# Attention probabilities turned by VectorE and a trip through memory; layer 1's gate path row-major

## The chip, the cores and the metric

The kernel runs on one NeuronCore of a Trainium2 chip. Its time is the device time of one execution in microseconds (us). TensorE multiplies matrices (a 128x128 stationary operand is loaded, then up to 512 columns stream past it), VectorE and ScalarE work element by element, GpSimd issues DMAs and a few small operations, SyncE issues the weight DMAs. All of them run side by side and wait for each other by semaphores.

## The reference, cut to what matters

A trunk of two layers on 256 tokens of width 2048, all in float32. Each layer is a token mixer, a gate, an output projection, a residual with layer norm, and a gated embedding:

```python
# layer 0: y = sgu_mixer(x, w_in_a)      u * (w_s @ LN(v) + b_s) * silu(z)
# layer 1: y = moba_mixer(x, w_in_b)
q, k, v, z = split(x @ w_in)             # 16 heads of 128
probs = softmax(causal(q @ k.T * 128 ** -0.5))     # 256 keys are one block: plain causal attention
y = (probs @ v) * silu(z)
# both layers
x = layer_norm(alpha * x + y @ w_out)
x = x + sigmoid(x @ w_ple_gate) * (p @ w_ple_proj)
```

With 256 tokens there is one key block, so the block selection of the second mixer drops out.

## The kernel before, in words

**Precision.** Every operand is split into a high part (rounded to TensorE's fp32r form, ScalarE, `split` L75 and L128) and a low part (the rest, VectorE, L76 and L129). A product is made of three matmuls: high by high, low by high, high by low.

**Weights.** They stream once through SBUF in chunks of 128x2048 numbers (1 MB). `load_weights` (L112) lets SyncE load a chunk in two halves and lets ScalarE and VectorE make its high and low part. `weights` (L132) keeps two chunks ready ahead of the one in use; there are three buffers for converted chunks. The list `chunks` (L93 to L108) gives the order and form of the chunks: `flat` for 128 output features by all 2048 inputs, `by_blocks` for 512 output features by 512 inputs.

**Two forms of a projection.** `row_slice` (L237) makes 512 output features for all tokens, token-major: tokens are the stationary operand, weights stream in 512 columns. It takes four `row_unit`s of one chunk each, each unit 24 matmuls of 512 columns (4 input tiles x 2 token tiles x 3). `column_unit` (L244) makes 128 output features feature-major from one chunk: weights are stationary, and the high and low part of the tokens stream. It takes 32 matmuls: 16 of 512 columns (both parts of the tokens at once) and 16 of 256. What follows a token-major result often needs it feature-major, so there are two ways to turn it: `turn` (L269) uses TensorE's transposes, `turn_far` (L283) uses VectorE's transposes of 32x32 blocks and lets two sets of DMAs (GpSimd's queue) put the blocks in place through a DRAM buffer: eight DMAs out, two back.

**Order of work.** The program is written out in one order and each engine executes its instructions in order. Each unit ends with `tick` (L167); `at(n, f, ...)` (L163) puts `f` after the n-th tick from then on. So smaller work lies between the units by tick counts written by hand.

**Layer 1's mixer.** After the values (L627 to L632) come 16 heads (L696): two column units make q and k of a head (`halves_sum`, then `split`). One tick later `scores` (L638) makes the masked scores (five matmuls), the row maxima, the exponentials and the normalised probabilities `sm`, token-major. Two ticks after that `probs` (L667) turns them: three 128x128 transposes on TensorE into a PSUM bank `pt`, then the split into high and low part `pb` (L673, L674). One tick later `values` (L677) multiplies by v and leaves the head's output `o` feature-major. After the heads, 16 column units make z feature-major (L703): two units, `halves_sum`, silu, times `o`, `split` into `br`. Then `after` (L470) multiplies `br` by w_out in four row slices, and so on.

**Layer 0's mixer** makes its z in another way (`gated`, L451): four row slices, silu, times `u`, and `turn_far` for the first three slices.

**Buffers.** `r4` (128x1024 floats) has 12 buffers, `t4` 20, `t2` 5, PSUM 8 banks.

Of the kernel before, what the change touches and what calls it, by code (L numbers as in the profile page):

```python
# [8 lines left out]
F32 = mybir.dt.float32  # L9
F32R = mybir.dt.float32r  # L10
AF = mybir.ActivationFunctionType
ALU = mybir.AluOpType

P = 128
D = 2048
S = 256
KT = D // P
NM = S // P
NS = D // 512
# [16 lines left out]
def f32(ap):  # L36
    return ap.bitcast(F32)
# [3 lines left out]
def decoder_trunk(ctx: ExitStack, tc: tile.TileContext, xT, pT, wv_a, wu_a, wz_a, w_sT, b_s,  # L41
# [5 lines left out]
    nc = tc.nc  # L47
# [4 lines left out]
    dram = ctx.enter_context(tc.tile_pool(name="dram", bufs=1, space=bass.MemoryType.DRAM))  # L52
    psum = ctx.enter_context(tc.tile_pool(name="psum", bufs=8, space=bass.MemoryType.PSUM))

    def t2(name):
        return act.tile([P, 512], F32, name=name, tag="t2", bufs=NT2)

    def t4(name):
        return act.tile([P, 1024], F32R, name=name, tag="t4", bufs=NT4)

    def r4(name):

        return act.tile([P, NM, 512], F32, name=name, tag="r4", bufs=NR4)

    def bank(name):
        return psum.tile([P, 512], F32, name=name, tag="bank", bufs=8)

    def in2(t):
        return t.rearrange("p (i s) -> p i s", i=2)

    def split(src, n="s", g=2):

        t = t4(n).rearrange("p (g h s) -> p g h s", g=g, h=2)
        src = src.rearrange("p (g s) -> p g s", g=g)
        nc.scalar.activation(t[:, :, 0, :], src, AF.Copy)  # L75
        nc.vector.tensor_sub(t[:, :, 1, :], src, f32(t[:, :, 0, :]))  # L76
        return t
# [4 lines left out]
    def by_blocks(w):  # L82

        return [("p (b k c) -> p k b c", dict(b=4, k=4),
                 w[4 * n:4 * n + 4, :, 512 * c:512 * c + 512].rearrange("b p e -> p b e"))
                for n in range(NS) for c in range(4)]

    def flat(src):
        return [("", {}, src.rearrange("p (b e) -> p b e", b=4))]
# [3 lines left out]
    chunks = []  # L93
    for k in range(KT):
        chunks += flat(wv_a[k])
    chunks += by_blocks(wu_a) + by_blocks(wz_a)
    for i in range(DEPTH):
        if i == 1:
            for h in range(2):
                for c in range(KT // 2):  # L100
                    chunks += flat(wv_b[h, c])
            for h in range(KT):
                chunks += flat(wqkz_b[h]) + flat(wqkz_b[KT + h])
            for f in range(KT):
                chunks += flat(wqkz_b[2 * KT + f])
        chunks += by_blocks(w_out[i])
        chunks += flat(w_proj[i, 0]) + flat(w_proj[i, 1])
        chunks += by_blocks(w_gate[i])  # L108
# [33 lines left out]
    ident = consts.tile([P, P], F32, name="ident")  # L142
# [20 lines left out]
    def at(units, f, *args):  # L163

        later.append([units, f, args])
# [71 lines left out]
    def row_slice(xs, name="y"):  # L237

        banks = [[bank(name)] for _ in range(NM)]
        for c in range(4):  # L240
            row_unit(banks, range(4 * c, 4 * c + 4), xs, both if c == 3 else None)
        return [b[0] for b in banks]

    def column_unit(xs, joined=False):  # L244


        ps = bank("f")
        wh, wl = (t.rearrange("p (k c) -> p k c", k=KT) for t in weights()[2:])
        for k in range(KT):
            feature_product(ps, wh[:, k, :], wl[:, k, :], xs, k, joined)  # L250
        tick()
        return ps
# [12 lines left out]
    def halves_sum(o, ps):  # L265
        nc.scalar.activation(o, ps[:, 0:S], AF.Copy)
        nc.vector.tensor_add(o, o, ps[:, S:2 * S])
# [12 lines left out]
        if keep is not None:  # L280
            nc.scalar.activation(keep[j // 2][:, j % 2, :], tp, AF.Copy)

    def turn_far(xs, n, rows, name):  # L283


        d = dram.tile([512, S], F32, name=f"{name}{n}")
        t = r4(name + "b")

        def block_turn():
            for m in range(NM):  # L290
                nc.vector.transpose(t[:, m, :], rows[n][:, m, :])  # L291
            for m in range(NM):
                for g in range(4):
                    c = slice(m * P + 32 * g, m * P + 32 * g + 32)
                    nc.gpsimd.dma_start(d[:, c].rearrange("(b c) t -> c b t", c=32),  # L295
                                        t[32 * g:32 * g + 32, m, :].rearrange("p (b t) -> p b t", t=32))

        def back():
            raw.append(r4(name + "r"))
            for j in range(2):  # L300
                nc.gpsimd.dma_start(in2(raw[0][:, j, :]),
                                    d[j * S:(j + 1) * S, :].rearrange("(u p) t -> p u t", p=P))

        def splits():
            for j in range(2):
                s = split(raw[0][:, j, :], name)
                xs[4 * n + 2 * j:4 * n + 2 * j + 2] = [s[:, u] for u in range(2)]

        raw = []
        block_turn()  # L310
        at(1, back)
        at(4, splits)
# [6 lines left out]
    xs = [None] * KT  # L319
# [125 lines left out]
    for n in range(NS):  # L445
        y = row_slice(xs, "u")
# [4 lines left out]
    def gated(o, xs):  # L451

        br = [None] * KT
        for n in range(NS):
            y = row_slice(xs, "z")
            for m in range(NM):
                t = t2("sz")
                nc.scalar.activation(t, y[m], AF.Silu)
                nc.vector.tensor_mul(o[n][:, m, :], o[n][:, m, :], t)
            if n < NS - 1:  # L460
                turn_far(br, n, o, "bt")
                continue
            for i in range(2):
                at(1 + i, turn, br, 2 * n + i, o, "b")
        return br

    br = gated(us, xs)
# [153 lines left out]
    xs = after(0, br)  # L621
# [12 lines left out]
    o = [None] * NS  # L634
    blocks = (slice(0, P), slice(P, 3 * P))
    w3 = slice(0, 3 * P)

    def scores(h, qk):  # L638
        qh, ql = qk[:, 0, 0, :], qk[:, 0, 1, :]
        kh, kl = qk[:, 1, 0, :], qk[:, 1, 1, :]  # L640
        c0, c1 = slice(0, P), slice(P, S)
        sc = bank("sc")

        t = sc.rearrange("p (a b) -> p a b", b=P)[:, 0:4:3, :]
        nc.tensor.matmul(t, qh[:, c0], qk[:, 1, :, c0], start=True, stop=False, skip_group_check=True)
        nc.tensor.matmul(sc[:, c0], ql[:, c0], kh[:, c0], start=False, stop=True, skip_group_check=True)
        t = sc[:, blocks[1]]
        nc.tensor.matmul(t, qh[:, c1], kh, start=True, stop=False, skip_group_check=True)
        nc.tensor.matmul(t, qh[:, c1], kl, start=False, stop=False, skip_group_check=True)
        nc.tensor.matmul(t, ql[:, c1], kh, start=False, stop=True, skip_group_check=True)  # L650
        s = t2("sm")
        nc.vector.tensor_add(s[:, w3], sc[:, w3], causal.rearrange("p a b -> p (a b)"))
        nc.vector.tensor_add(s[:, c0], s[:, c0], sc[:, 3 * P:4 * P])
        mx = small.tile([P, NM], F32, name="mx")
        sm = small.tile([P, NM], F32, name="sum")
        for m in range(NM):
            nc.vector.tensor_reduce(mx[:, m:m + 1], s[:, blocks[m]], axis=mybir.AxisListType.X, op=ALU.max)
        nc.vector.tensor_scalar(mx, mx, -QK_SCALE, None, op0=ALU.mult)
        for m in range(NM):
            nc.scalar.activation(s[:, blocks[m]], s[:, blocks[m]], AF.Exp, scale=QK_SCALE,  # L660
                                 bias=mx[:, m:m + 1], accum_out=sm[:, m:m + 1])
        nc.vector.reciprocal(sm, sm)
        for m in range(NM):
            nc.vector.tensor_scalar(s[:, blocks[m]], s[:, blocks[m]], sm[:, m:m + 1], None, op0=ALU.mult)
        at(2, probs, h, s)

    def probs(h, s):  # L667
        tp = bank("pt")
        for b in range(3):
            nc.tensor.transpose(tp[:, b * P:(b + 1) * P], s[:, b * P:(b + 1) * P], ident)  # L670

        p = t4("pb").rearrange("p (h s) -> p h s", h=2)
        nc.scalar.activation(p[:, 0, w3], tp[:, w3], AF.Copy)  # L673
        nc.vector.tensor_sub(p[:, 1, w3], tp[:, w3], f32(p[:, 0, w3]))  # L674
        at(1, values, h, p)

    def values(h, p):  # L677
# [15 lines left out]
    def head(h, t):  # L693
        at(1, scores, h, split(t, "qk"))

    for h in range(KT):  # L696
        t = t2("qk")
# [2 lines left out]
        head(h, t)  # L700

    br = [None] * KT
    for j in range(KT // 2):  # L703
        t = t2("sz")
        for u in range(2):
            halves_sum(t[:, u * S:(u + 1) * S], column_unit(xs))
        nc.scalar.activation(t, t, AF.Silu)
        nc.vector.tensor_mul(t, t, o[j // 2][:, j % 2, :])
        t = split(t, "b")
        br[2 * j:2 * j + 2] = [t[:, u] for u in range(2)]  # L710
# [57 lines left out]
```

## Time and profile before

| | before |
|---|---|
| median of 3 runs | 1041.56 us (1041.35 to 1041.69) |
| the profiled execution's own time | 1041.33 us |
| its span, first to last instruction | 1039.6 us |
| TensorE matmul busy | 1032.2 us (99%) |
| VectorE busy | 653.2 us (63%) |
| ScalarE busy | 492.2 us (47%) |
| GpSimd busy | 84.0 us (8%) |
| TensorE clock granted | 1.000 of full speed |
| DMA | 211.24 MB, mean 203 GB/s |

The span is the time between the first and the last instruction of the program; 1.7 us of the execution lie outside it. Busy time of an engine is the union of its records. Matmul records overlap, since the engine is pipelined: a 512-column matmul's record is 389 ns long, but the next one starts some 227 ns later. What TensorE really needs is therefore read from the distance between starts.

### The profile page before, as it was taken

How to read it: one execution, taken by the hardware profiler on the slowest of the kernel's cores; microseconds unless marked ns; L12 is line 12 of the kernel's file. 1: busy time of each engine (PE TensorE's matmuls, PEld its weight loads, DVE VectorE, ACT ScalarE, POOL GpSimd, SP SyncE). 2: the span in 40 equal slices, each digit the busy share in tenths (PEclk: the TensorE clock that was granted, in tenths of full speed). 3: DMA queues.
4: the chain of work that ended last, by engine and by line, in shares of the span. 5: the costliest groups of instructions: out<-in, count | busy, mean ns of one | idle time of the engine just before them, and what ended most of it. 6: DMA issues, size and time to landing. Idle time of an engine off the chain costs nothing.

```text
span 1039.6 us, 13497 instructions
## 1 busy us (share of the span) xinstructions
PE 1032.2 (99%) x5134; PEld 873.0 (84%) x5134; DVE 653.2 (63%) x855; ACT 492.2 (47%) x672; POOL 84.0 (8%) x140
## 2 busy tenths in 40 slices
PE   9999999999999999999999999999999999999998
PEld 7888888888888878888888888888888888888887
DVE  5646765566475696665545666666665655669564
ACT  6535454444353364543435555555554553346442
POOL 1000100033300002224000000000000000000221
PEclk9999999999999999999999999999999999999999
DMA  8855787678865546778755555555545565555672
GB/s 309 284 202 181 245 230 210 195 210 266 304 212 202 195 168 194 254 240 274 237 189 189 168 172 170 163 164 170 172 164 188 178 212 192 193 184 170 214 220 44
DMA packets 102753, 211.24 MB, mean 203 GB/s; under 512 B 25456, under 2 KB 26496, under 8 KB 102688
## 3 DMA queue, kind: packets, MB, share of 16 engines
q1 hardware_dynamic: 96848, 194.93, 57.1%
q0 software_dynamic: 5696, 15.32, 5.5%
q8 instruction: 40, 0.66, 0.2%
q14 instruction: 25, 0.20, 0.1%
q10 hardware_dynamic: 144, 0.13, 0.0%
HBM read 204.53 MB, written 5.82 MB: 202 GB/s over the span
## 4 chain that ended last, share of the span: by engine, by line
issue 44%; PE 9%; DMA 3%; DVE 2%; POOL 1%; ACT 0%; POOLq 0%; DVEq 0%
PE g L262 2%; PE g L223 2%; PE g L221 2%; PE g L219 2%; DMA xtr<-xt 2%; DMA xt<-xtb 1%; DVE wl L129 0%; POOL xt L295 0%; PE tp L276 0%; DVE xt L76 0%; DVE sg L569 0%; DVE r L570 0%; DVE xtb L291 0%; ACT xt L75 0%; POOL rs L491 0%
## 5 line engine op out<-in xcount | busy, mean ns | idle before, releaser
L129 DVE TENSOR_TENSOR wl<-wr,wh 128x1024 fp32r<-128x1024 f32 (+1 forms) x363 | 431.2, 1211 | 268.7 <-ACT wh L128 265.0
L128 ACT ACTIVATE wh<-wr 128x1024 fp32r<-128x1024 f32 (+1 forms) x363 | 370.4, 1047 | 386.6 <-PE y L221 127.0
L262 PE MATMUL f<-xt,wh 128*128 128x512 f32 x768 | 271.0, 396 | 0.0
L262 PE MATMUL f<-xt,wl 128*128 128x256 f32 x768 | 206.2, 279 | 0.0
L262 PEld LDWEIGHTS f<-xt,wh 128*128 128x128 f32 x768 | 143.2, 188 | 29.9
L262 PEld LDWEIGHTS f<-xt,wl 128*128 128x128 f32 x768 | 144.5, 188 | 2.9
L219 PE MATMUL g<-wh,xn 128*128 128x512 f32 x224 | 87.9, 393 | 0.0
L223 PE MATMUL g<-wl,xn 128*128 128x512 f32 x224 | 87.2, 389 | 0.0
L221 PE MATMUL g<-wh,xn 128*128 128x512 f32 x224 | 87.2, 389 | 0.0
L219 PE MATMUL y<-wh,b 128*128 128x512 f32 x160 | 62.2, 389 | 0.0
L221 PE MATMUL y<-wh,b 128*128 128x512 f32 x160 | 62.2, 389 | 0.0
L223 PE MATMUL y<-wl,b 128*128 128x512 f32 x160 | 62.2, 389 | 0.0
L219 PE MATMUL u<-wh,x 128*128 128x512 f32 x128 | 49.9, 390 | 0.0
L221 PE MATMUL u<-wh,x 128*128 128x512 f32 x128 | 49.9, 390 | 0.0
L219 PE MATMUL z<-wh,x 128*128 128x512 f32 x128 | 49.8, 389 | 0.0
L221 PE MATMUL z<-wh,x 128*128 128x512 f32 x128 | 49.8, 389 | 0.0
L223 PE MATMUL u<-wl,x 128*128 128x512 f32 x128 | 49.8, 389 | 0.0
L223 PE MATMUL z<-wl,x 128*128 128x512 f32 x128 | 49.8, 389 | 0.0
L223 PEld LDWEIGHTS g<-wl,xn 128*128 128x128 f32 x224 | 42.0, 188 | 8.8
L221 PEld LDWEIGHTS g<-wh,xn 128*128 128x128 f32 x224 | 42.1, 188 | 8.5
L219 PEld LDWEIGHTS g<-wh,xn 128*128 128x128 f32 x224 | 42.1, 188 | 8.4
L491 POOL TENSOR_TENSOR rs<-rs,half 128x2 f32<-128x2 f32 x2 | 2.3, 1146 | 541.2 <-DVE rs L490 541.2
(178 smaller groups left out, 1514.3 us busy)
## 6 DMA issues: line engine op xcount, KB each, us to landing
wr<-in_wqkz_b SPq DMA_DIRECT2D x96, 512.0 KB, 3.6
wr<-in_w_out SPq DMA_DIRECT2D x64, 512.0 KB, 4.3
wr<-in_w_gate SPq DMA_DIRECT2D x64, 512.0 KB, 4.2
wr<-in_wu_a SPq DMA_DIRECT2D x32, 512.0 KB, 4.6
wr<-in_wz_a SPq DMA_DIRECT2D x32, 512.0 KB, 5.0
wr<-in_wv_b SPq DMA_DIRECT2D x32, 512.0 KB, 4.7
wr<-in_wv_a SPq DMA_DIRECT2D x30, 512.0 KB, 5.0
gb<-vecs POOLq DMA_DIRECT2D x24, 256.0 KB, 7.9
```

What stands on the lines that cost most here:

```text
L128: nc.scalar.activation(hi[:, c], raw, AF.Copy)
L129: nc.vector.tensor_sub(lo[:, c], raw, f32(hi[:, c]))
L219: nc.tensor.matmul(o(n), xh, wh[i][n], start=first, stop=False, skip_group_check=NN == NS)
L221: nc.tensor.matmul(o(n), xl, wh[i][n], start=False, stop=False, skip_group_check=NN == NS)
L223: nc.tensor.matmul(o(n), xh, wl[i][n], start=False, stop=last, skip_group_check=NN == NS)
L262: nc.tensor.matmul(*m, start=k == 0 and j == 0, stop=k == KT - 1 and j == len(ms) - 1, skip_group_check=True)
L491: nc.gpsimd.tensor_tensor(rs, rs, half, op=ALU.pow)
```

## The change

Probabilities: `probs` no longer uses TensorE. VectorE transposes the 32x32 blocks of the 128x384 probabilities into one half of an `r4` tile, GpSimd issues four DMAs (32 partitions each, runs of 32 numbers) to a DRAM buffer, and one tick later one DMA back, which brings them in turned. Two ticks after that they are split, with the same two instructions as before but from SBUF instead of PSUM. `probs` comes one tick after `scores` instead of two; the values come after five ticks instead of three.

z of layer 1: the first 12 of its 16 chunks are `by_blocks`, and three row slices make 1536 of the 2048 features token-major, with silu from PSUM into an `r4` tile and `turn_far`. In `turn_far` the turned z is multiplied by the head outputs `o` before its split. The last 512 features stay with the column units.

```diff
@@ chunks
-            for f in range(KT):
+            chunks += by_blocks(wqkz_b[2 * KT:2 * KT + 12])
+            for f in range(12, KT):
                 chunks += flat(wqkz_b[2 * KT + f])
@@ turn_far
-    def turn_far(xs, n, rows, name):
+    def turn_far(xs, n, rows, name, times=None):
...
         def splits():
             for j in range(2):
+                if times is not None:
+                    nc.vector.tensor_mul(raw[0][:, j, :], raw[0][:, j, :], times[n][:, j, :])
                 s = split(raw[0][:, j, :], name)
@@ scores
-        at(2, probs, h, s)
+        at(1, probs, h, s)
 
     def probs(h, s):
-        tp = bank("pt")
-        for b in range(3):
-            nc.tensor.transpose(tp[:, b * P:(b + 1) * P], s[:, b * P:(b + 1) * P], ident)
+        d = dram.tile([3 * P, P], F32, name=f"pt{h}")
+        t = r4("pt")
+        nc.vector.transpose(t[:, 0, w3], s[:, w3])
+        for g in range(4):
+            nc.gpsimd.dma_start(d[:, 32 * g:32 * g + 32].rearrange("(b c) q -> c b q", c=32),
+                                t[32 * g:32 * g + 32, 0, w3].rearrange("p (b q) -> p b q", q=32))
+        at(1, probs_back, h, d, t)
+
+    def probs_back(h, d, t):
+        nc.gpsimd.dma_start(t[:, 1, w3].rearrange("p (b q) -> p b q", b=3), d.rearrange("(b p) q -> p b q", p=P))
+        at(2, probs_split, h, t)
+
+    def probs_split(h, t):
         p = t4("pb").rearrange("p (h s) -> p h s", h=2)
-        nc.scalar.activation(p[:, 0, w3], tp[:, w3], AF.Copy)
-        nc.vector.tensor_sub(p[:, 1, w3], tp[:, w3], f32(p[:, 0, w3]))
+        nc.scalar.activation(p[:, 0, w3], t[:, 1, w3], AF.Copy)
+        nc.vector.tensor_sub(p[:, 1, w3], t[:, 1, w3], f32(p[:, 0, w3]))
         at(1, values, h, p)
@@ z of layer 1
-    for j in range(KT // 2):
+    sz = [None] * (NS - 1)
+    for n in range(NS - 1):
+        y = row_slice(xs, "z")
+        sz[n] = r4("sz")
+        for m in range(NM):
+            nc.scalar.activation(sz[n][:, m, :], y[m], AF.Silu)
+        turn_far(br, n, sz, "z", o)
+    for j in range(6, KT // 2):
         t = t2("sz")
```

## Rows read from the trace of the kernel before

**Rows 1.** The page: engines' busy time, and TensorE's granted clock by slices.

```profile
PE 1032.2 (99%) x5134; PEld 873.0 (84%) x5134; DVE 653.2 (63%) x855; ACT 492.2 (47%) x672; POOL 84.0 (8%) x140
...
PEclk9999999999999999999999999999999999999999
```

**Rows 2.** Waits of PE: us in total, times, longest us.

```profile
PE tp L276 <- DVE r L380: 1.1, 2, 0.6
PE warm L317 <- DVE ones L141: 1.1, 1, 1.1
...
```

**Rows 3.** PE's timeline (start, length in us) between two column units: scores alone.

```profile
569.57 0.28 PE L645 MATMUL sc<-qk 128*128 128x256 f32 x1
...
570.16 0.40 PE L262 MATMUL f<-xt,wh 128*128 128x512 f32 x1
```

**Rows 4.** The same later: transposes, then scores.

```profile
657.00 0.49 PE L670 MATMUL pt<-ident,sm 128*128 128x128 f32 x3
...
657.92 0.40 PE L262 MATMUL f<-xt,wh 128*128 128x512 f32 x1
```

**Rows 5.** The same after the last head: transposes alone.

```profile
770.46 0.49 PE L670 MATMUL pt<-ident,sm 128*128 128x128 f32 x3
770.71 0.48 PE L262 MATMUL f<-xt,wh 128*128 128x512 f32 x1
```

**Rows 6.** Window of nine column units of z: length, PE busy (records), clock, DMA.

```profile
788.14:839.02 50.88, 50.88 (x290) 1.00 0.55 186
```

**Rows 7.** Window of the 384 matmuls of the values (`y<-xt`, row units).

```profile
465.62:552.62 87.00, 87.00 (x384) 1.00 0.72 232
```

**Rows 8.** Window of layer 0's z, its 384 row matmuls alone.

```profile
185.80:275.03 89.23, 87.58 (x384) 1.00 0.78 234
```

**Rows 9.** Window with one `turn_far` trip: length, busy of PE, PEld, DVE, ACT, POOL.

```profile
445.00:468.00 23.00, 23.00 (x103) 19.06 (x102) 14.75 (x18) 11.35 (x14) 6.60 (x10) 1.00 0.77 236
```

**Rows 10.** Timeline of that trip, all engines.

```profile
448.56 0.71 DVE L291 STREAM_TRANSPOSE xtb<-r 128x512 f32<-128x512 f32 x1
...
449.57 2.57 POOL L295 DMA_DIRECT2D xt<-xtb  x4 [1.59 <-DVE xtb L291]
...
457.95 0.72 POOL L301 DMA_DIRECT2D xtr<-xt  x1 [5.81 <-DMA xt<-xtb]
...
463.88 0.63 ACT L75 ACTIVATE xt<-xtr 128x512 fp32r<-128x512 f32 x1 [1.75 <-DMA xtr<-xt]
```

**Rows 11.** Tile `xtb`: durations in ns min/median/max, and landings.

```profile
L295 POOL DMA_DIRECT2D xt<-xtb x32: 648/649/712, 401.2 to 474.2; - x32
...
DMA to landing us min/median/max: 2.3/3.9/5.7
```

**Rows 12.** Tile `xtr`, the way back.

```profile
DMA to landing us min/median/max: 4.0/5.4/6.7
```

**Rows 13.** Tile `pb`, the split of the probabilities.

```profile
L673 ACT ACTIVATE pb<-pt x16: 471/475/481, 582.6 to 771.9; 128x384 fp32r<-128x384 f32 x16
L674 DVE TENSOR_TENSOR pb<-pt,pb x16: 549/551/552, 583.8 to 773.2; 128x384 fp32r<-128x384 f32 x16
```

**Rows 14.** Window of 28 column units of the heads, all engines.

```profile
582.28:758.77 176.49, 176.49 (x1080) 156.50 (x1079) 120.70 (x238) 92.50 (x183) 0.00 (x0) 1.00 0.51 168
```

**Rows 15.** Timeline of one head's end of scores and the next unit's start.

```profile
651.41 0.55 DVE L664 TENSOR_SCALAR sm<-sm,sum 128x128 f32<-128x128 f32 x2
...
657.25 1.06 ACT L128 ACTIVATE wh<-wr 128x1024 fp32r<-128x1024 f32 x1 [3.11 <-issue]
658.21 0.47 ACT L673 ACTIVATE pb<-pt 128x384 fp32r<-128x384 f32 x1
...
658.58 1.05 ACT L128 ACTIVATE wh<-wr 128x1024 fp32r<-128x1024 f32 x1
```

**Rows 16.** Tile `sz`, layer 1's gate path: durations in ns min/median/max.

```profile
L267 DVE TENSOR_TENSOR sz<-sz,f x16: 408/421/422, 761.3 to 845.3; 128x256 f32<-128x256 f32 x16
...
L708 DVE TENSOR_TENSOR sz<-sz,o x8: 683/685/691, 768.1 to 847.4; 128x512 f32<-128x512 f32 x8
```

More of the change, by code (lines that the diff above doesn't have):

```diff
@@ L85, in by_blocks @@
                  w[4 * n:4 * n + 4, :, 512 * c:512 * c + 512].rearrange("b p e -> p b e"))
-                for n in range(NS) for c in range(4)]
+                for n in range(w.shape[0] // 4) for c in range(4)]
     def flat(src):
```

## The prediction, made before the run

> **What bounds the kernel now.** I read the page's busy times first: TensorE's matmuls fill 99% of the span, VectorE 63%, and the clock is granted in full in every slice [rows 1]. Since matmul records overlap, that 99% proves little by itself, so the waits come next: TensorE waits in four places, 3.2 us in all, the longest 1.1 us, at the start and at the transposes behind the layer norms (the two rows left out are 0.5 us each, in the first stage) [rows 2]. Nowhere near the heads or z does it wait for anything. So the end is set by the sum of the distances between matmul starts, and the change is worth what it takes off that sum, less what it makes TensorE wait.
>
> **Part 1: the probabilities' transposes leave TensorE.** The timeline of TensorE between two column units shows the price. Where only scores lie between them, the next unit starts 570.16 - 569.57 = 0.59 us after the first score matmul [rows 3]. With three transposes ahead, it starts 657.92 - 657.00 = 0.92 us after the first transpose [rows 4]. The transposes therefore cost 0.33 us: 0.25 for themselves and 0.08 because the first score matmul behind them moves on later. This pattern occurs for heads 1 to 15, each of which has the transposes of the head before it in its tick; the last head's transposes stand alone and cost 770.71 - 770.46 = 0.25 us [rows 5]. Sum: 15 x 0.33 + 0.25 = 5.2 us off the path. Bounds: 16 x 0.25 = 4.0 if the 0.08 stays, 16 x 0.33 = 5.3 at most. I take 5.2. Nothing takes their place on TensorE, and the PSUM bank is no longer needed.
>
> [...]
>
> **Part 2: three slices of z row-major.** A column unit of z without small work beside it takes 50.88 / 9 = 5.653 us (288 matmuls; two neighbours reach into the window) [rows 6]. A row unit has 24 matmuls of 512 columns; 384 of them with the same tokens as operand take 87.00 us, so a unit takes 24 x 87.00 / 384 = 5.438 us [rows 7]. The streamed columns are as many in both (24 x 512 = 16 x 768); the column form is slower per column. Twelve units: 12 x 0.215 = 2.6 us off the path. Lower bound from layer 0's z, the same unit form with `by_blocks` chunks: 87.58 / 384 x 24 = 5.474, so 12 x 0.18 = 2.1 [rows 8]. I take 2.6. `turn_far` adds no matmul.
>
> **What is added, and its cover.** For VectorE: a transpose of 128x384 per head. The trace has 0.71 us for 128x512 [rows 10]; I take three quarters, 0.53 us, with 0.71 as the upper end. VectorE is busy 120.70 of 176.49 us there, 68% [rows 14]; 14 x 0.53 = 7.4 us more make it 73%. The split keeps its two instructions, 0.475 and 0.551 us [rows 13]; from SBUF I take the same. For each slice of z, two block transposes (1.42 us) replace VectorE's part of four `halves_sum` (4 x 0.42 = 1.7); the products with `o` and the splits keep number and size [rows 16]. ScalarE loses its four copies. All of it lies beside matmuls, and costs nothing while the waits below keep their slack; without that cover it is 0.53 us per head, 8.5 us.
>
> GpSimd, which does nothing during the heads [rows 14], issues five DMAs per head, 5 x 0.65 = 3.3 us [rows 11] of some 12.3 us per head. Its queue stands still while the way back waits for the way out; only the next head's DMAs are behind that. Behind z's trips stand only the gain and bias loads of the last stage, due many units later. No weight load changes place on SyncE's queue, only the form of twelve chunks.
>
> DMA traffic: 16 x 2 x 197 KB and 3 x 2 x 524 KB are 9.4 MB over some 284 us, 33 GB/s on top of 168 to 191 [rows 6, 14]. A window with a trip under way moved 236 GB/s, and TensorE was busy for all of its 23.00 us [rows 9].
>
> **The new wait.** Per head: transposes, four DMAs out, landing, one back, landing, split. The whole trip of `turn_far` is in the trace: its block transposes end at 448.56 + 0.71 = 449.27, the first use of the data starts at 463.88, 14.6 us, with eight DMAs of 64 KB and two of 256 KB [rows 10]. A head's trip has four of 48 KB and one of 192 KB. Lower end: 0.3 to the first issue, 4 x 0.65, a median landing of 3.9 and one of 5.4: 12.2 us [rows 10 to 12]. Upper end with the longest landings seen, 5.7 and 6.7, and 0.5 before the way back: 15.8. I take 14, near the whole row. In the written order the split comes three units after the transposes. A unit of the heads with its small work took 176.49 / 28 = 6.30 us, and will take about 6.14 without the transposes; three are 18.4 us. So VectorE's loop, 0.53 + 14 = 14.5, fits with some 4 us to spare. TensorE needs the result a further unit later. ScalarE may reach the split (L673) early and stand there: the probabilities are ready late (the scaling of a head runs at 651.41, near the end of the unit after its scores), and ScalarE does a tick's work at the start of a unit [rows 15]. Queued behind it are the second half of a weight conversion and a `halves_sum`; ScalarE is idle 3.1 us before each conversion in that very pattern [rows 15], and the converted chunk is the one two units ahead. I cost this at nothing.
>
> For z: the split is four units behind the block transposes, 21.8 us, against a trip of 14.6; layer 0 does the same and has no TensorE wait in its z [rows 2, 8]. The last trip's split falls beside the last column unit; its `br` is used two row units later, 10.9 us on.
>
> **Sum.** The profiled execution took 1041.33 us, span 1039.6 and 1.7 around it. 1041.33 - 5.2 - 2.6 = 1033.5; the median of the runs stands 0.23 above that execution, so 1033.8 us, 0.75% faster. Own range: from 1033.8 with the lower ends (4.0 + 2.1), 1035.5, to some 1032.5, since a shorter head phase shifts small overlaps by tenths.
>
> **Rivals.**
> 1. *The trip is too long, and the heads run at its pace* (slower). VectorE executes in order: when a head's split waits for its landing, the next heads' transposes wait too, so three units cannot be shorter than transposes plus trip. Place: L673/L674 in the heads. It starts to cost at a trip of 17.9 us and eats the whole gain at 18.6 (10.7 such loops in 16 heads, 0.73 us each). At 20 us: 10.7 x 2.1 = 22 us, 1056. For it: 128-byte runs and five dependent DMAs. Against it: 14.6 us for more data, and 15.8 with the longest landings [rows 10 to 12]. Chance 6%.
> [...]
> 2. *Half of the gain is given back*: ScalarE standing at L673 delays a weight conversion or a `halves_sum` by just enough that TensorE waits 0.25 us per head, 4 us: 1037.8. For it: L673 lies between the two halves of a conversion [rows 15]. Against it: two chunks ready ahead. Chance 8%.
> 3. [...] Chance 1%.
> 4. *The freed time does not show*, since something other than TensorE's sum sets the end, so within 0.2% of before: 1041. Against it: the waits of TensorE. Chance 3%.
>
> **How the numbers follow.** The forecast has 82%. The range 1031.8 to 1038.0 takes in the forecast with its bounds and rival 2, about 88% less what bounds off by some tenths may cost, so some 8 in 10. 0.2% of 1041.56, 2.1 us, is about what a measurement can tell here. Faster by more: forecast, rivals 2 and 3, 91%, less a little for rivals 2 and 4 running into each other: 0.89. Same: 0.04. Slower: rival 1 and an unknown wait, 0.07.
>
> **What would show it.** Right: between column units of the heads 0.59 us where scores lie and never 0.92; twelve row units of 5.44 us in z; no group of TensorE waits at scores, `ov` or `f`; from a head's block transposes to its split 12 to 16 us. Wrong: waits of TensorE for `pb` or for `wh`/`wl` in the heads; a wait of ScalarE for the probabilities' landing of more than some 5 us per head; row units in z slower than in the values' stage.

## The result, and the profile after

| | before | changed |
|---|---|---|
| median of 6 runs each, on one chip | 1041.45 us (1041.20 to 1041.69) | 1034.53 us (1034.05 to 1035.01) |
| ratio, 95% interval | | 0.9933 (0.9922 to 0.9943) |
| profiled execution, its span | 1041.33, 1039.6 us | 1034.86, 1033.2 us |

The change saves 6.9 us, 0.67%. The forecast was 1033.8 us, 7.8 us less than before. The direction, the place and the larger of the two terms came as predicted; 0.7 us of the smaller one did not come. The page of the changed kernel answers to [rows 1]:

```profile
PE 1025.6 (99%) x4990; PEld 865.0 (84%) x4990; DVE 662.1 (64%) x865; ACT 490.8 (48%) x660; POOL 156.0 (15%) x250
...
PEclk9999999999999999999999999999999999999999
```

TensorE has 144 matmuls less: 48 transposes, and 12 x 8 from twelve units that take 24 matmuls instead of 32. GpSimd's busy time nearly doubles, VectorE's grows by 9 us, and TensorE is as full as before, at a granted clock of 0.999 on average. So the first question is whether it waits anywhere new. These are its waits in the changed kernel (us in all, times, longest), beside [rows 2]:

```profile
PE tp L277 <- DVE r L383: 1.1, 2, 0.6
PE warm L320 <- DVE ones L142: 1.1, 1, 1.1
PE v L220 <- ACT wh L129: 0.6, 1, 0.6
PE v L224 <- DVE wl L130: 0.5, 1, 0.5
```

The same four places, none in the heads or in z. So the time can be read from the distances between matmul starts. First TensorE's timeline between two column units of the heads (start, length):

```profile
642.85 0.28 PE L648 MATMUL sc<-qk 128*128 128x256 f32 x1
...
643.43 0.39 PE L263 MATMUL f<-xt,wh 128*128 128x512 f32 x1
```

643.43 - 642.85 = 0.58 us with scores alone, in every head; the 0.92 of [rows 4] is gone. The window of twelve column units of the heads, the answer to [rows 14]:

```profile
661.79:735.43 73.64, 73.64 (x447) 65.66 (x446) 55.76 (x108) 40.51 (x80) 19.25 (x31) 1.00 0.66 203
```

73.64 / 12 = 6.14 us for a unit with its small work, where it was 176.49 / 28 = 6.30; the prediction had 6.14. VectorE's share went from 68% to 76% (73% predicted, with the added time set against the old length of the window), DMA from 168 to 203 GB/s (33 GB/s more predicted, 35 came).

The added work, by the tile `pt` (durations in ns, min/median/max):

```profile
L677 POOL DMA_DIRECT2D pt<-pt x64: 616/618/642, 578.1 to 765.5; - x64
L675 DVE STREAM_TRANSPOSE pt<-sm x16: 570/578/580, 577.3 to 762.8; 128x384 f32<-128x384 f32 x16
L682 POOL DMA_DIRECT2D pt<-pt x16: 748/753/759, 584.8 to 770.3; - x16
L688 ACT ACTIVATE pb<-pt x16: 513/520/527, 591.0 to 774.7; 128x384 fp32r<-128x384 f32 x16
L689 DVE TENSOR_TENSOR pb<-pt,pb x16: 549/550/559, 592.5 to 775.3; 128x384 fp32r<-128x384 f32 x16
```

The landings of its DMAs, way out and way back (size of one, median us from issue to landing):

```profile
pt<-pt POOLq DMA_DIRECT2D x64, 48.0 KB, 2.3
pt<-pt POOLq DMA_DIRECT2D x16, 192.0 KB, 4.8
```

And one head's trip in the timeline, all engines:

```profile
660.66 0.58 DVE L675 STREAM_TRANSPOSE pt<-sm 128x384 f32<-128x384 f32 x1
...
661.53 2.45 POOL L677 DMA_DIRECT2D pt<-pt  x4 [3.95 <-DVE pt L675]
...
665.99 0.75 POOL L682 DMA_DIRECT2D pt<-pt  x1 [2.01 <-DMA pt<-pt]
...
671.13 0.40 ACT L663 ACTIVATE sm<-sm,mx 128x128 f32<-128x128 f32 x1 [1.20 <-DVE mx L661]
...
672.93 0.58 DVE L675 STREAM_TRANSPOSE pt<-sm 128x384 f32<-128x384 f32 x1
...
676.69 0.52 ACT L688 ACTIVATE pb<-pt 128x384 fp32r<-128x384 f32 x1
...
683.40 0.40 ACT L663 ACTIVATE sm<-sm,mx 128x128 f32<-128x128 f32 x1 [1.20 <-DVE mx L661]
```

The block transposes end at 661.24. The way back is issued 4.75 us later; by the record of that DMA it landed 10.5 us after the transposes (9.1 to 13.0 over the 16 heads, 10.0 in the median). ScalarE comes to the split at 676.69, 15.45 us after the transposes, and the row has no wait behind it: the data had been there for 5 us. Only for the last two heads does ScalarE wait, 8.5 us in all, and nothing is late by it.

Last, the row units of z. The columns are those of [rows 14]: length, busy of PE, PEld, DVE, ACT, POOL, clock, DMA:

```profile
788.42:815.62 27.20, 27.20 (x122) 22.52 (x121) 14.10 (x16) 12.70 (x15) 6.79 (x11) 1.00 0.69 231
...
759.81:765.36 5.55, 5.55 (x26) 4.56 (x26) 3.05 (x5) 2.69 (x4) 1.71 (x3) 1.00 0.33 106
```

The last five units take 27.20 / 5 = 5.440 us each, as predicted. But the unit from 759.81 takes 5.55. What is different there is what lies ahead of it, the `ov` matmuls of a head. Part of the missing 0.7 us is in such units; the rest is in the column units that went, as worked out below.

**The balance.** Compared by starts in the two traces: the heads and z took 292.05 us before and 285.01 after, 7.04 less. The stage ahead of them, the same code in both, ended 0.59 us later in the changed kernel's profiled execution (553.21 against 552.62 at the first column unit), and the rest, to the last matmul, took 190.86 and 190.85. 7.04 - 0.59 = 6.45, and the executions differ by 1041.33 - 1034.86 = 6.47. That 0.59 is scatter: a later trace of the same kernel (e11 below) has 552.37.

### The profile page after: what moved, and what is told of

It reads as the page before. It is cut to its first block, busy times and chain, and to the rows that moved or that the text cites. A ratio compares the mean times of both kernels' runs of the same rounds, so it can differ in the third digit from the quotient of the medians.

```text
span 1033.2 us, 13402 instructions
## 1 busy us (share of the span) xinstructions
PE 1025.6 (99%) x4990; PEld 865.0 (84%) x4990; DVE 662.1 (64%) x865; ACT 490.8 (48%) x660; POOL 156.0 (15%) x250
## 4 chain that ended last, share of the span: by engine, by line
PE 67%; issue 19%; DMA 8%; DVE 2%; POOL 2%; ACT 1%; SPq 0%; POOLq 0%; DVEq 0%; ACTq 0%
PE f L263 17%; PE g L224 5%; PE g L220 5%; PE g L222 5%; PE u L222 3%; PE u L220 3%; PE y L222 3%; PE y L224 3%; PE y L220 3%; PE u L224 3%; PE v L224 3%; PE v L222 3%; PE v L220 3%; PE g L263 2%; DMA pt<-pt 2%
## 5 line engine op out<-in xcount | busy, mean ns | idle before, releaser
L263 PE MATMUL f<-xt,wh 128*128 128x512 f32 x576 | 203.5, 394 | 0.0
L263 PE MATMUL f<-xt,wl 128*128 128x256 f32 x576 | 155.5, 280 | 0.0
L263 PEld LDWEIGHTS f<-xt,wh 128*128 128x128 f32 x576 | 107.4, 187 | 21.5
L263 PEld LDWEIGHTS f<-xt,wl 128*128 128x128 f32 x576 | 108.8, 189 | 2.0
L677 POOL DMA_DIRECT2D pt<-pt x64 | 39.4, 621 | 191.3 <-DVE pt L675 190.7
L224 PE MATMUL y<-wl,xt 128*128 128x512 f32 x128 | 40.7, 389 | 0.0
L222 PE MATMUL y<-wh,xt 128*128 128x512 f32 x128 | 40.7, 389 | 0.0
L220 PE MATMUL y<-wh,xt 128*128 128x512 f32 x128 | 40.7, 389 | 0.0
```

The source lines that it names most:

```text
L220: nc.tensor.matmul(o(n), xh, wh[i][n], start=first, stop=False, skip_group_check=NN == NS)
L222: nc.tensor.matmul(o(n), xl, wh[i][n], start=False, stop=False, skip_group_check=NN == NS)
L224: nc.tensor.matmul(o(n), xh, wl[i][n], start=False, stop=last, skip_group_check=NN == NS)
L263: nc.tensor.matmul(*m, start=k == 0 and j == 0, stop=k == KT - 1 and j == len(ms) - 1, skip_group_check=True)
L677: nc.gpsimd.dma_start(d[:, 32 * g:32 * g + 32].rearrange("(b c) q -> c b q", c=32), t[32 * g:32 * g + 32, 0, w3].rearrange("p (b q) -> p b ...
```

## The experiments

Ratios are against the kernel before, run on the same chip, with 95% intervals. The three groups ran on three chips, where the kernel before had medians of 1041.26 (e1 to e4), 1041.36 (e5 to e8) and 1041.53 us (e9 to e12).

### Each half alone, and the trip without its gain

**e1_probs_only**: the new probabilities, z as before.

```diff
-            chunks += by_blocks(wqkz_b[2 * KT:2 * KT + 12])
-            for f in range(12, KT):
+            for f in range(KT):
...
-    for j in range(6, KT // 2):
+    for j in range(KT // 2):
```

> Only the first part: the probabilities go by VectorE and memory, z stays in 16 column units. Theory (TensorE's sum of start distances sets the time and the new trip is covered): 5.2 us less than before, 1036.2. Rival (the trip costs TensorE some tenths per head and z gives the full 2.6): 1037 to 1038.

Measured: 1036.33 us, 0.9952 (0.9940 to 0.9964), 4.9 us less; heads and z 286.84 us, 5.21 less. As expected.

**e2_z_only**: the new z, the probabilities by TensorE as before.

```diff
-        at(1, probs, h, s)
+        at(2, probs, h, s)
...
+            nc.tensor.transpose(tp[:, b * P:(b + 1) * P], s[:, b * P:(b + 1) * P], ident)
```

> Only the second part: z in three row slices and one of column units, the probabilities turned by TensorE as before. In the profile of the changed kernel the twelve row units take 5.440 us where nothing precedes them, but 5.51 and 5.55 behind scores or values, while the column units that they replace were shortened to 5.56 and 5.61 by the same neighbours. Theory (this is why z was over-priced): 1.7 us less than before, 1039.7. Rival (z gives its 2.6 and the shortfall lies with the heads): 1038.8.

Measured: 1039.52 us, 0.9983 (0.9975 to 0.9992), 1.7 us less; heads and z 290.21, 1.84 less. The halves add up: 5.21 + 1.84 = 7.05, and both together gave 7.04.

**e3_unused_transposes**: the changed kernel, with three TensorE transposes per head whose result nobody reads.

```diff
         at(1, probs_back, h, d, t)
+        at(1, unused, s)
+
+    def unused(s):
+        tp = bank("pu")
+        for b in range(3):
+            nc.tensor.transpose(tp[:, b * P:(b + 1) * P], s[:, b * P:(b + 1) * P], ident)
```

> The changed kernel, and TensorE also makes the three transposes of each head as before, into a bank that nobody reads. The trip through memory stays. Theory (the gain of the heads is TensorE's time for the transposes alone): 5.2 us slower than the changed kernel, 1039.7, the same as with z alone. Rival (the trip itself costs something): slower than z alone by that cost.

Measured: 1039.39 us, 0.9980 (0.9971 to 0.9989). That is e2 to within 0.13 us, though e3 has the whole trip and e2 has none of it; heads and z take 290.29 us in e3 and 290.21 in e2. So the transposes were worth what they occupied, and VectorE's transposes, 80 DMAs and the later split cost nothing that can be measured.

### How much room the trip has

**e5_split_one_earlier**: the split one tick earlier, two units behind the probabilities instead of three.

```diff
     def probs_back(h, d, t):
...
-        at(2, probs_split, h, t)
+        at(1, probs_split, h, t)
```

> The changed kernel with the split of the probabilities one unit after the transposes' DMAs back are issued instead of two, so two units after the transposes and the values four ticks after the scores. In the changed kernel a head's trip takes 9.1 to 13.0 us, some 10 at the median, and ScalarE comes to the split 15.5 us after the transposes. Theory (the written order leaves more than 5 us unused): no TensorE wait, 1034.5. The prediction's loop rule (transposes plus trip must fit into the units between): 10.7 against 12.3 us, also 1034.5. Rival (ScalarE's and VectorE's standing at the split costs at once): 2 us per head, 1060 or more.

Measured: 1060.19 us, 1.0173 (1.0156 to 1.0190). The theory and the loop rule of the prediction both fell; the rival was right. Waits of ScalarE, then of TensorE, in this kernel:

```profile
ACT pb L688 <- DMA pt<-pt: 101.1, 16, 8.8
```

```profile
PE sc L648 <- DVE qk L76: 15.3, 8, 3.1
PE ov L700 <- ACT pb L688: 1.9, 1, 1.9
```

ScalarE stands at the split in every head. Its timeline, with VectorE's and GpSimd's, from one head's transposes to the next one's:

```profile
716.02 0.58 DVE L675 STREAM_TRANSPOSE pt<-sm 128x384 f32<-128x384 f32 x1
...
724.38 0.76 POOL L682 DMA_DIRECT2D pt<-pt  x1 [4.51 <-DMA pt<-pt]
...
729.36 0.53 ACT L688 ACTIVATE pb<-pt 128x384 fp32r<-128x384 f32 x1 [8.41 <-DMA pt<-pt]
729.79 0.39 ACT L663 ACTIVATE sm<-sm,mx 128x128 f32<-128x128 f32 x1
...
731.58 0.58 DVE L675 STREAM_TRANSPOSE pt<-sm 128x384 f32<-128x384 f32 x1
```

L663, right behind the split, holds the exponentials of the next head. They wait for the trip of this head, and the next head's transposes wait for them. So a loop closes over one head: transposes, trip, split, exponentials, scaling, transposes. It takes 731.58 - 716.02 = 15.6 us here, one of the longest, where a head's matmuls take 73.64 / 6 = 12.27. By the trace the loop sets the pace from the third head on: each of the 13 distances to the next head's transposes (12.7 to 16.0 us) is the time from the end of this head's transposes to its split, plus 2.8 us. Behind the split also stands ScalarE's part of a q and k (L267, L75), for which the scores wait (15.3 us).

In the changed kernel the split of a head stands behind the exponentials of the next head and ahead of those of the one after that: in the timeline above, L663 at 671.13 belongs to the transposes at 672.93, the next ones, and it runs ahead of the split at 676.69. The exponentials of the one after that start at 683.40, behind it. The loop closes over two heads, 24.5 us. One tick decides which.

Behind some of TensorE's waits in e5 the next unit was longer too. Windows of the unit behind the longest wait, of the one after it, and of the unit behind a wait of 2.9 us:

```profile
662.27:669.84 7.57, 7.57 (x33) 6.53 (x33) 3.84 (x9) 1.05 (x3) 0.76 (x1) 0.71 0.83 282
669.84:675.49 5.65, 5.65 (x33) 4.90 (x32) 4.79 (x9) 4.11 (x9) 2.46 (x4) 1.00 0.17 36
735.07:742.20 7.13, 7.13 (x33) 6.13 (x33) 4.32 (x10) 1.44 (x3) 0.76 (x1) 0.77 0.89 283
```

TensorE had stood for 3.1 us, and the unit behind it ran at a granted clock of 0.71 on average and took 7.57 us; the one after it took 5.65 at 1.00. The unit behind the wait of 2.9 us took 7.13 us at 0.77, and the one behind the wait of 1.9 us at `ov` took 7.11. Behind a wait of 2.8 us, at 718.78, the unit took 5.65 us (719.45 to 725.10). In the first of these units the first two matmuls of 512 columns start 662.91 - 662.27 = 0.64 us apart, in the last 719.79 - 719.45 = 0.34:

```profile
662.27 0.63 PE L263 MATMUL f<-xt,wh 128*128 128x512 f32 x1
...
662.91 0.63 PE L263 MATMUL f<-xt,wh 128*128 128x512 f32 x1
```

```profile
719.45 0.39 PE L263 MATMUL f<-xt,wh 128*128 128x512 f32 x1
...
719.79 0.40 PE L263 MATMUL f<-xt,wh 128*128 128x512 f32 x1
```

Why the clock was lower behind some waits and not behind another, no run shows.

**e6_split_two_earlier**: the split in the tick of the way back.

```diff
-        at(2, probs_split, h, t)
+        probs_split(h, t)
```

> The same with the split in the tick in which the way back is issued, one unit after the transposes, and the values two ticks after the transposes. Theory (TensorE waits only when the values' turn comes before the probabilities are there, and VectorE has other work to do meanwhile): the trip's 10 us and 1.1 us of split against 12.3 us to the values, so TensorE waits 0 to 1 us at some heads, 1035 to 1042. The prediction's loop rule: 10.7 us of transposes and trip in one unit of 6.1 costs 4.5 us per head, 72 us, 1107.

Measured: 1047.58 us, 1.0054 (1.0040 to 1.0069). Neither number was met; the theory's was nearer. The split stands ahead of the next head's exponentials here too, and TensorE waits for it:

```profile
PE ov L700 <- ACT pb L688: 9.1, 6, 2.4
...
PE ov L700 <- DVE pb L689: 1.0, 5, 0.2
```

But the way back landed 8.6 to 12.8 us after the transposes, in nine of 16 heads below 10, with a median of 9.6 over all heads, against 9.9 to 13.2 and a median of 11.5 in e5. Successive transposes are mostly 12 to 15 us apart, so many heads keep up with the matmuls (12.27) and some do not. The way back landed 3.3 us after its issue in e6 and 4.6 in e5, in the median; why the trips are shorter in e6 was not settled.

**e9_back_late**: the way back issued late. A one-column VectorE copy from a later head's q or k into its target holds it back, and the split follows in the same tick.

```diff
-        at(1, probs_back, h, d, t)
+        at(3, probs_back, h, d, t)
...
     def probs_back(h, d, t):
+        nc.vector.tensor_copy(t[:, 1, 0:1], latest[0])
...
-        at(2, probs_split, h, t)
+        probs_split(h, t)
...
+            latest[0] = t[:, j * S:j * S + 1]
```

> The changed kernel, its ticks for split and values unchanged, but the way back of each head is held until a head's sums of the third unit after the transposes are made (a copy of one column ahead of it, into the buffer that it fills), so that the data land some 18 us after the transposes instead of 10. Theory (in the changed kernel the split of a head stands ahead of the exponentials of the next head but one, so the loop has two heads, 24.5 us, for the trip and some 3 us of softmax): no TensorE wait, 1034.5 to 1035. The prediction's rule (transposes and trip within three units, 18.4 us): 0.2 to 1 us per loop, 1036 to 1045. Rival (any wait of ScalarE at the split costs, as in the run with the split one unit earlier): 1050 or more.

Measured: 1034.31 us, 0.9931 (0.9918 to 0.9945), the changed kernel's time. In the trace the way back is issued 12.9 to 16.3 us after the transposes in the first 14 heads and lands after 15.8 to 21.3 us. TensorE has the four waits of the changed kernel and no other; ScalarE does wait at the split:

```profile
ACT pb L689 <- DMA pt<-pt: 16.8, 11, 5.7
```

8.9 us of these fall on the last two heads, whose trips were not lengthened, as 8.5 do in the changed kernel.

The two-head loop held, the prediction's rule did not: for 10 of 16 heads the trip was longer than the 17.9 us from which it was to cost, and it cost nothing. A trip of 21.3 us and the 2.8 us of split, exponentials, scaling and transposes found in e5 still fit 24.5 us. e5 and e9 together show the limit to be the place of the split in ScalarE's order, not the length of the trip against the units between. That the loop runs through the exponentials is read from the order and the distances in e5; no run moved them alone.

### The missing 0.7 us, and the rest of z

**e10_late_values**: the values of the last three heads are held back until z's row units are over, so that no `ov` lies between them.

```diff
-        at(1, values, h, p)
+        at({13: 11, 14: 10, 15: 9}.get(h, 1), values, h, p)
```

> The changed kernel with the values' matmuls of the last three heads moved from between z's row units to beside z's last four column units. Theory (a row unit behind values takes 5.55 instead of 5.44 us, a column unit behind them 5.61 instead of 5.65): 3 x 0.11 + 0.05 + 3 x 0.04 = 0.5 us less, 1034.0; in the profile all row units behind the first two at 5.44. Rival (the difference goes with z's first units, whatever stands between them): no change, 1034.5.

Measured: 1034.24 us, 0.9930 (0.9918 to 0.9942); the changed kernel had 1034.32 on the same chip. The times can't tell the two apart; the trace can. Windows of five row units, from the second behind the last scores on, of which the changed kernel has three at 5.55, and of the first of them:

```profile
758.87:786.07 27.20, 27.20 (x122) 22.52 (x120) 14.18 (x17) 13.24 (x15) 8.36 (x13) 1.00 0.65 204
758.87:764.31 5.44, 5.44 (x26) 4.50 (x24) 2.83 (x6) 2.42 (x3) 1.17 (x2) 1.00 0.33 119
```

Without `ov` ahead of them all five take 27.20 / 5 = 5.440. So the 5.55 came from the neighbour. By the trace 0.27 us of the 0.5 expected is gained, heads and z together take 284.74 against 285.01: the three column units that now have the `ov` ahead of them take 5.70 us instead of 5.65, where less than 5.65 was expected.

**e4_all_rows**: the last slice of z row-major too, with its splits after three ticks.

```diff
...
+            chunks += by_blocks(wqkz_b[2 * KT:2 * KT + KT])
...
-        at(4, splits)
+        at(wait, splits)
...
+        turn_far(br, n, sz, "z", o, 3 if n == NS - 1 else 4)
...
```

> The last slice of z is row-major too and turned through memory; its split comes three units after its end, ahead of the output projection's fourth unit, which is the first to need it. Theory (the turned slice of the trace arrives some 25 us after its row slice ends, three units cover 16.3): TensorE waits 6 to 10 us at that unit and gains 0.8 in the slice, so 1040 to 1044. Rival (the trip of 14.6 us is covered but for 1 or 2 us): 1034.5 to 1036.

Measured: 1035.19 us, 0.9950 (0.9937 to 0.9962). The theory of a long wait was wrong, the rival's range was met; heads and z take 284.17, 0.84 less. What eats it is a wait in the output stage, whose 384 matmuls take 88.95 us instead of 87.05; the list of waits has 1.1 of these 1.9 us:

```profile
PE y L218 <- ACT z L75: 1.1, 1, 1.1
```

VectorE's timeline there:

```profile
836.21 0.69 DVE L306 TENSOR_TENSOR zr<-zr,o 128x512 f32<-128x512 f32 x1 [1.69 <-DMA zr<-z]
837.45 0.69 DVE L306 TENSOR_TENSOR zr<-zr,o 128x512 f32<-128x512 f32 x1 [0.54 <-DMA zr<-z]
838.06 0.70 DVE L290 STREAM_TRANSPOSE zb<-sz 128x512 f32<-128x512 f32 x1
```

The last slice's transposes stand in VectorE's order behind the products of slice 2, which wait for their own trip.

**e7_all_rows_order**: e4 with slice 2's splits one tick later, behind those transposes.

```diff
-        turn_far(br, n, sz, "z", o, 3 if n == NS - 1 else 4)
+        turn_far(br, n, sz, "z", o, (4, 4, 5, 3)[n])
```

> All four slices of z row-major, as in the run before, but the split of the third slice comes one tick later. There VectorE stood at the product of the third slice, whose data were not back, for 1.7 and 0.5 us, and the last slice's block transposes stood behind it: the first silu was done at 834.6, its transposes began at 838.1. Theory (that order made the last trip late): the transposes begin 2 us earlier, TensorE's wait at the output projection's fourth unit, 1.9 us, goes to 0 to 0.3, and the slice's 0.85 us are left as a gain on the changed kernel: 1033.5 to 1034.0. Rival (the trip itself is too long for three units): the wait stays above 1 us, 1034.5 to 1035.5.

Measured: 1033.69 us, 0.9931 (0.9919 to 0.9942). The first of the transposes starts at 836.28 instead of 838.06, TensorE's wait is out of the list, and the output stage's matmuls take 87.19 us:

```profile
836.28 0.70 DVE L290 STREAM_TRANSPOSE zb<-sz 128x512 f32<-128x512 f32 x1
```

By time e7 and the changed kernel can't be told apart; their intervals nearly coincide.

**e8_all_far**: e7, and layer 0's last slice by `turn_far` as well.

```diff
-            if n < NS - 1:
-                turn_far(br, n, o, "bt")
-                continue
-            for i in range(2):
-                at(1 + i, turn, br, 2 * n + i, o, "b")
+            turn_far(br, n, o, "bt", wait=(4, 4, 5, 3)[n])
```

> As the run before, and layer 0's last z slice is turned through memory too, with the same ticks, instead of by eight TensorE transposes in two ticks. There two blocks of four transposes stand between 280.493 and 280.846 and between 286.417 and 286.771, and layer 0's first four output units take 88.01 us where 384 plain row matmuls take 87.05. Theory: 0.9 us less than the run before, 1032.6 to 1033.1. Rival (layer 0's stage has more DMA traffic, so its last slice comes too late): TensorE waits 1 us or more at the fourth unit there, no gain.

Measured: 1032.57 us, 0.9914 (0.9901 to 0.9927). Layer 0's 384 output matmuls take 87.22 us, where eight transposes among them made it 88.01:

```profile
274.69:361.91 87.22, 87.22 (x385) 71.98 (x384) 51.99 (x55) 35.55 (x39) 10.78 (x18) 1.00 0.70 232
```

**e11_changed_again** and **e12_all_far_again**: the changed kernel and e8, side by side with the kernel before.

> The changed kernel once more, beside the next one: 1034.5 as before.

> The kernel that turns all z slices of both layers through memory, once more, beside the changed kernel: 1.5 us less than that by the profiles (0.7 in layer 1, 0.8 in layer 0), 1033.0; measured before 1032.6.

Measured: 1034.32 us, 0.9931 (0.9919 to 0.9944), and 1032.88 us, 0.9921 (0.9907 to 0.9934). The intervals against the kernel before overlap; the difference of the medians, on one chip, is 1.44 us. The distances in the traces of the changed kernel and of e12 give 0.84 (heads and z) and 0.82 (layer 0's output matmuls, 87.19 us), less 0.16 in layer 1's output stage (87.21 against 87.05), 1.50 in all.

## Why the prediction was right, and where it was off

**The bound.** "The end is set by the sum of the distances between matmul starts" held: the balance above closes to 0.02 us, and in e3 the trip with all its work moved nothing.

**Part 1, the transposes: right.** 5.2 us predicted. The gaps between units fell from 0.914 to 0.583 us in fifteen places and by 0.244 once: 15 x 0.331 + 0.244 = 5.21. e1 measured 4.9 by time and 5.21 by its trace. Rival 3, by which they are worth the length of their records, is out with that: in the trace of before the 48 records are 271 ns long in the median, 13.0 us in all, and it is the distance of starts that was saved, 5.21 us.

```profile
L670 PE MATMUL pt<-ident,sm x48: 270/271/273, 581.4 to 770.7; 128*128 128x128 f32 x48
```

**Part 2, z: mechanism right, size off.** This is the term that failed: 12 x 0.215 = 2.6 us predicted, 1.84 by the trace of e2, 1.74 by its time. I took both unit lengths from stretches without small work between the units [rows 6, 7]. The twelve units that went lay elsewhere. In the trace of before they start at 752.25, beside the last heads' scores, transposes and `ov`, and five of them are shorter than 5.653: 5.606, 5.558, 5.606, 5.641 and 5.610 us. All twelve took 67.59 us, not 12 x 5.653 = 67.84. In the changed kernel five of the twelve row units are longer than 5.440, those behind scores and `ov` by 0.05 to 0.11: 65.74 us, not 12 x 5.438 = 65.26. 0.25 + 0.48 = 0.73, and 2.58 - 0.73 = 1.85. The lower bound of 2.1 had 5.474 us for a row unit, from [rows 8], and 65.74 / 12 = 5.478 came; it was too high by the column units alone.

**The cover: right.** VectorE's transposes took 578 ns (530 taken), GpSimd's issues 618 and 753 ns (650 taken), ScalarE's split from SBUF 520 ns (475 taken, as from PSUM), all beside matmuls. By the tile's rows above none of the 64 issues took more than 642 ns, in heads where VectorE was busy for 55.76 of 73.64 us, 76%.

**The trip: covered, but over-estimated.** 14 us taken, with 12.2 as the lower end; 10.0 measured in the median. The landings were the reason: 2.3 us for 48 KB and 4.8 for 192 KB, where I had put 3.9 and 5.4 from DMAs of 64 and 256 KB [rows 11, 12]. That is 2.2 us less, all of 12.2 - 10.0.

**The loop rule: wrong in form, without harm to the number.** The prediction wanted the trip to fit three units and put rival 1 at 17.9 us. e9 ran with trips of up to 21.3 us for nothing, and e5, whose split had two units, lost 25.9 us against the changed kernel (1060.19 - 1034.32, medians on two chips) though its trips, 11.5 us in the median, were shorter than two units (12.3) in 12 of 16 heads. What counts is which head's exponentials stand behind the split on ScalarE. The prediction looked for the loop on VectorE and took what is queued on ScalarE for a conversion and a `halves_sum` only, though the softmax of a head is there too. Rival 1 was therefore one tick away in the written order, not 4 us of trip. That the written order had the split on the safe side of those exponentials was luck: the prediction had not asked.

**Rivals 2 and 4** did not come: no wait of TensorE in the heads, and the time fell by more than the 0.2% that can be told.

## What to carry to other kernels

On this full TensorE (99% busy) the change was worth the distance between starts that it removed: 5.21 us for transposes with 13.0 us of records. That distance is to be taken from the very units that go and come, with their neighbours, not from a clean stretch of the same form, which gave 2.6 us for z where 1.84 came. Here work that was moved from the full engine to idle ones and to a long trip cost nothing that can be measured (e3 and e2 differ by 0.13 us) as long as the instruction that waits for the trip stood, in its engine's order, behind what the next round needs: look at each engine that waits for the trip, and write down what is queued behind the wait. Where a hand-written delay can differ by one unit, a run with one unit less shows how near the edge is: here it lost 25.9 us, while trips of up to 21.3 us instead of some 10 cost nothing in e9.

## What the runs showed of the hardware

- The length of a run of matmuls went with its neighbours, beyond the small work's own time: a column unit took 5.653 us among its like, 5.61 and 5.55 in the heads, and 5.70 behind `ov` in e10; a row unit 5.440, and 5.55 behind `ov`. e10 shows for the row units that it is the `ov`; what in TensorE makes it was not tried.
- A wait of 3.1 us of TensorE in e5 was followed by a unit of 7.57 us at a mean granted clock of 0.71, and one of 2.9 us by a unit of 7.13 at 0.77, where a unit at 1.00 took 5.65; a wait of 2.8 us in the same run was followed by a unit of 5.65 us.
- Turning 192 KB by VectorE's block transposes, four DMAs to memory and one back took 10.0 us in the median beside the stream of weights; `turn_far`'s 512 KB took 14.6 in the one trip shown [rows 10].
- ScalarE copied 128x384 numbers in 520 ns from SBUF and in 475 ns from PSUM [rows 13]; VectorE's subtraction took 550 from either.
